# Five elementwise operations of the top-k bias, for blocks 1 to 4, on GpSimd instead of VectorE

## The chip, the core and the metric

The kernel runs on one core of a Trainium2 chip. The metric is the device time of one execution in microseconds, the median of the runs shown.

## What is computed

One layer of a hybrid decoder. After an RMSNorm and one input projection, two groups of heads attend. The first is multi-head latent attention, dense and causal. The second is sparse: an indexer scores all keys, each query keeps its 256 best causal keys, and softmax attention runs over those alone. Then come the output projection, a residual, a SwiGLU feed-forward network with its residual, and a last RMSNorm. The part that matters here is the choice of the keys:

```python
score = jnp.where(causal[None], score, -jnp.inf)
_, sel = lax.top_k(score, topk)          # topk = 256
valid = sel <= qpos[None, :, None]
...
s = jnp.einsum('bqhd,bqkhd->bhqk', qb, k_sel, ...) * scale
s = jnp.where(valid[:, None], s, -jnp.inf)
p = jax.nn.softmax(s, axis=-1)
```

## The kernel before

There are 1024 tokens in eight query blocks of 128, and 16 meta tokens in front of the keys, so block b has 16 + 128(b+1) keys (`n_keys`). The kernel does not gather. For each block it turns the scores into a row of biases, 0 for a kept key and 1e30 for the others, and the attention scores of the sparse heads are all computed and get that bias (`scores`, L792). Block 0 needs only the causal bias.

**From scores to bias.** `idx_block` sums the eight indexer heads into `sc[b]` (128 x keys, fp32) and `keys` splits each score into an ordered high half `hi[b]` and low half `yb[b]`, both 16 bits wide and stored in the place of the score. `topk` then searches bit by bit: `search` counts in 16 steps how many high halves reach a trial value, L436 to L440 prepare the low halves of the ties, and a second search of 16 steps finds the low threshold `q`. Blocks 1 and 2 are searched together on VectorE (L397 to L406), blocks 3 and 4 one after the other on ScalarE (L382 to L385, with a last small step on GpSimd, L389 and L390).

**The end of `topk`**, L445 to L458, makes the bias once per block, on a block's 272 (block 1), 400, 528 or 656 (block 4) columns. L445 counts the keys above the low threshold and L446 takes them off what is needed. L448 marks low halves equal to `q`, L449 keeps those with the threshold's high half, L451 numbers them with a prefix sum, and L452 keeps the first `need` of them. L453 marks low halves above `q`, L454 adds both marks, L455 adds the high halves above the threshold, L457 turns a mark into 0 or 1e30, and L458 adds the causal bias to the last 128 columns. All are VectorE's. The tiles `e` and `g` and the search's own output (`jk`, from `junk`, L411) take turns in a ring of two buffers; the numbering of L451 lies in `g`, so L453 can write `g` only after L452 has read it.

**Order.** Nothing of the order is written by hand: the program is given to a scheduler that fixes each engine's queue when the kernel is built, by its own estimate of when things are ready. Each engine then works through its queue in order and waits at its head.

The stages, by the time at which they run in the profiled execution:
- to about 328 us the projections. `run` (L588) works through seven column groups of the input matrix, each for eight row blocks, in a ring of seven PSUM banks once the first groups are done; ScalarE copies the products out, VectorE rotates them (`rope`, L334 to L336), GpSimd adds the halves (L338) and takes the low parts of the weights (L191). Top-k of blocks 1 to 4 is mixed into this stage by `fill` (`TOPK`, L47), and ends in the next.
- from about 328 us the latent projections and attention of blocks 0 to 2 (`CFG_A`). Their sparse heads read the biases of blocks 1 and 2, copied at L970; those of blocks 3 and 4 are copied at L1327 and first read by the second attention.
- from about 500 to 1050 us three streams side by side: the attention of blocks 3 to 7 (`CFG_B`), the feed-forward network of blocks 0 to 2 (`ffn`), and the top-k of blocks 5 to 7 (`TOPK_B`, `DEFER`).
- then the output projection and the feed-forward network of blocks 3 to 7, to the end.

Of the kernel before, what the change touches and what calls it, by code (L numbers as in the profile page):

```python
# [19 lines left out]
OP = mybir.AluOpType  # L20
# [6 lines left out]
P = 128  # L27
# [3 lines left out]
NK = NM + T  # L31
# [16 lines left out]
DEFER = (5, 6, 7)  # L48
# [35 lines left out]
BIG = 1e30  # L84
# [6 lines left out]
def n_keys(b):  # L91
    return NM + P * (b + 1)
# [13 lines left out]
def hybrid_layer(ctx, tc, a, out):  # L106
    nc = tc.nc
    V, S, G, PE = nc.vector, nc.scalar, nc.gpsimd, nc.tensor
# [20 lines left out]
    cbias = cp.tile([P, NK], BF, name="cbias")  # L129
# [102 lines left out]
    yb = {b: sc[b].bitcast(U16)[:, n_keys(b):2 * n_keys(b)] for b in sc}  # L232
# [7 lines left out]
    with ExitStack() as es:  # L240
# [170 lines left out]
        def junk(n):  # L411
            return wk_pool[0].tile([P, NK], BF, name="jk", bufs=2)[:, :n]
# [11 lines left out]
        def topk(blocks, on_act):  # L424
# [17 lines left out]
            q = yield from search(blocks, yb, 32768.0, w[:, 4:8], on_act, thr[:, 1:2] if on_act else need)  # L442
            for b, c, n in cols:
                yield
                V.tensor_scalar(junk(n), yb[b], q[:, c], None, op0=OP.is_gt, op1=OP.add, accum_out=cnt[:, c])  # L445
                V.tensor_sub(need[:, c], need[:, c], cnt[:, c])  # L446
                e, g = junk(n), junk(n)
                V.tensor_scalar(e, yb[b], q[:, c], None, op0=OP.is_equal)  # L448
                V.scalar_tensor_tensor(e, hi[b], Th[:, c], e, op0=OP.is_equal, op1=OP.mult)  # L449
                rk = g.bitcast(F16)  # L450
                V.tensor_tensor_scan(rk, e, e, 0.0, OP.add, OP.bypass)  # L451
                V.scalar_tensor_tensor(e, rk, need[:, c], e, op0=OP.is_le, op1=OP.mult)  # L452
                V.tensor_scalar(g, yb[b], q[:, c], None, op0=OP.is_gt)  # L453
                V.tensor_add(e, e, g)  # L454
                V.scalar_tensor_tensor(g, hi[b], Th[:, c], e, op0=OP.is_gt, op1=OP.add)  # L455
                bb = yb[b].bitcast(BF)
                V.tensor_scalar(bb, g, -BIG, BIG, op0=OP.mult, op1=OP.add)  # L457
                V.tensor_tensor(bb[:, n - P:n], bb[:, n - P:n], cbias[:, NK - P:NK], op=OP.add)  # L458
                yield

        def start(groups, on_act, steps):
# [197 lines left out]
    op = ctx.enter_context(tc.tile_pool(name="oh", bufs=1))  # L659
# [647 lines left out]
    with aa_es:  # L1307
        work = attention(aa, BLK_A, cfg)
        rest = mla_rest()
        n = 0  # L1310
# [57 lines left out]
    for x, y in ((ckH, ckL), (wkH, wkL)):  # L1368
        n = x.shape[1] // WO_W
# [55 lines left out]
```

## Time and profile before

| | |
|---|---|
| median of 3 runs | 1516.27 us (1514.63 to 1522.13) |
| profiled execution | 1515.98 us |
| its span in the trace | 1514.2 us |
| TensorE matmul busy | 1405.1 us, 93% |
| VectorE busy | 1105.3 us, 73% |
| ScalarE busy | 922.9 us, 61% |
| GpSimd busy | 892.8 us, 59% |

The span is from the first to the last instruction of the core; the execution's own time holds 1.8 us more. Busy times of engines overlap. A group of instructions in the profile is told by its line in the kernel, its engine, what it writes from what it reads, and its shape; the idle time beside it is that of its engine just before. PE is TensorE, DVE VectorE, ACT ScalarE, POOL GpSimd.

### The profile page before, as it was taken

What the parts mean: (1) busy time and instruction counts of PE and PEld (TensorE: products, weight loads), DVE (VectorE), ACT (ScalarE), POOL (GpSimd) and SP (SyncE); (2) the same over time, 40 slices, a digit from 0 to 9 for tenths busy, and PEclk for the clock granted to TensorE, in tenths of its full rate; (3) what the DMA queues carried; (4) which work ended last, traced back from release to release, by engine and by line L of the source; (5) the groups of instructions that cost most, each with busy time, mean ns of one, the idle gap of its engine ahead of it and who ended that gap; (6) DMA issues with size and microseconds to landing.
All of it is one profiled execution on the core that took longest, in us unless ns stands there. A gap on an engine that the chain in (4) does not pass through costs nothing. (4 is left out here: it accounts for less than half of the span.)

```text
span 1514.2 us, 29979 instructions
## 1 busy us (share of the span) xinstructions
PE 1405.1 (93%) x10320; PEld 1295.3 (86%) x10320; DVE 1105.3 (73%) x2714; ACT 922.9 (61%) x2264; POOL 892.8 (59%) x1185
## 2 busy tenths in 40 slices
PE   6999998899989899899999999888799999999996
PEld 5999998897778789798888888788789999999995
DVE  6878989948886875957766666736676777777766
ACT  5666578897889889788544444434544444444444
POOL 2564555212404588687878778643846666666653
PEclk9999999999999799999999999998899999999999
DMA  6113265224434688687879998741222222222211
GB/s 177 55 48 85 73 143 134 52 89 131 130 102 123 146 193 166 147 171 175 182 157 222 200 203 181 188 140 50 65 62 84 84 84 84 79 76 83 84 56 70
DMA packets 353737, 180.74 MB, mean 119 GB/s; under 512 B 196560, under 2 KB 341344, under 8 KB 353584
## 3 DMA queue, kind: packets, MB, share of 16 engines
q1 hardware_dynamic: 353584, 178.82, 47.7%
q8 instruction: 81, 1.33, 0.4%
q14 instruction: 72, 0.59, 0.1%
HBM read 120.77 MB, written 21.30 MB: 94 GB/s over the span
## 5 line engine op out<-in xcount | busy, mean ns | idle before, releaser
L191 POOL TENSOR_TENSOR wL<-raw,wH 128x256 fp32r<-128x256 f32 x352 | 286.1, 846 | 59.0 <-ACT wH L188 55.3
L821 POOL TENSOR_TENSOR hl<-pd,hl 128x260 f16<-128x260 f32 (+5 forms) x256 | 168.8, 689 | 71.1 <-ACT hl L817 31.8
L191 POOL TENSOR_TENSOR wsl<-raw,wsh 128x256 fp32r<-128x256 f32 x132 | 120.3, 940 | 94.1 <-ACT wsh L188 53.6
L196 PE MATMUL b<-wh,uH 128*128 128x256 f32 (+3 forms) x568 | 169.2, 298 | 6.3 <-DVE mlo L318 3.2
L198 PE MATMUL b<-wh,uL 128*128 128x256 f32 (+3 forms) x568 | 168.5, 297 | 0.0
L197 PE MATMUL b<-wl,uH 128*128 128x256 f32 (+3 forms) x568 | 168.1, 296 | 0.1
L188 ACT ACTIVATE wH<-raw 128x1024 fp32r<-128x1024 f32 x88 | 91.8, 1054 | 79.4 <-PE b L198 20.0
L196 PE MATMUL b<-us,wsh 128*128 128x320 f32 x440 | 136.1, 313 | 1.5 <-DVE oh L1251 1.1
L197 PE MATMUL b<-us,wsh 128*128 128x320 f32 x440 | 136.4, 311 | 0.0
L198 PE MATMUL b<-us,wsl 128*128 128x320 f32 x440 | 134.2, 310 | 0.0
L196 PE MATMUL b<-ua,wH 128*128 128x384 f32 x352 | 122.1, 347 | 3.4 <-ACT wH L188 3.4
L382 ACT ACTIVATE js<-sc,bs 128x528 bf16<-128x528 int16 (+7 forms) x128 | 120.9, 945 | 4.7 <-DVE sc L437 2.4
L197 PE MATMUL b<-ua,wH 128*128 128x384 f32 x352 | 121.2, 344 | 0.0
L198 PE MATMUL b<-ua,wL 128*128 128x384 f32 x352 | 120.7, 344 | 0.1
L196 PE MATMUL b<-wH,hH 128*128 128x512 f32 x282 | 113.5, 403 | 3.9 <-DVE oh L1171 2.1
L196 PEld LDWEIGHTS b<-wh,uH 128*128 128x128 f32 x568 | 108.7, 191 | 8.3 <-DVE mlo L318 3.9
L197 PE MATMUL b<-wL,hH 128*128 128x512 f32 x282 | 112.1, 397 | 0.0
L198 PE MATMUL b<-wH,hL 128*128 128x512 f32 x282 | 110.1, 398 | 0.4 <-DVE hL L193 0.4
L197 PEld LDWEIGHTS b<-wl,uH 128*128 128x128 f32 x568 | 108.8, 191 | 0.5 <-DVE wl L193 0.3
L198 PEld LDWEIGHTS b<-wh,uL 128*128 128x128 f32 x568 | 108.6, 191 | 0.4 <-DVE uL L193 0.2
L1240 DVE TENSOR_TENSOR oh<-b,oh 128x512 f32<-128x512 f32 x110 | 74.5, 685 | 46.3 <-PE b L198 45.4
L799 ACT ACTIVATE pd<-pd,sm 128x528 f32<-128x528 f32 (+4 forms) x80 | 75.7, 946 | 48.6 <-DVE sm L797 46.1
(410 smaller groups left out, 4848.0 us busy)
## 6 DMA issues: line engine op xcount, KB each, us to landing
raw<-in_w_gate SPq DMA_DIRECT2D x44, 512.0 KB, 4.0
raw<-in_w_up SPq DMA_DIRECT2D x44, 512.0 KB, 4.1
raw<-in_w_down SPq DMA_DIRECT2D x44, 512.0 KB, 3.7
wor<-in_w_o SPq DMA_DIRECT2D x64, 128.0 KB, 2.5
wraw<-in_w_in SPq DMA_DIRECT2D x40, 128.0 KB, 2.4
vh<-v_x SPq DMA_DIRECT2D x16, 288.0 KB, 3.8
xt<-in_x SPq DMA_DIRECT2D x8, 512.0 KB, 4.4
ks_x<-st SPq DMA_DIRECT2D x32, 128.0 KB, 2.1
```

The source lines that it names most:

```text
L188: S.activation(h, src, AF.Copy)
L191: G.tensor_sub(l[:, c], src[:, c], h[:, c])
L196: PE.matmul(o, lh, rh, start=first, stop=False, **kw)
L197: PE.matmul(o, lh, rl, start=False, stop=False, **kw)
L198: PE.matmul(o, ll, rh, start=False, stop=last, **kw)
L382: S.activation(act_junk()[:, :n_keys(b)], y[b], AF.Sign, bias=cols[0], accum_out=cnt)
L799: S.activation(pb, pb, AF.Exp, bias=mn, scale=-1.0, accum_out=z)
L821: G.tensor_sub(pl_[:, c], pb[:, c], ph[:, c])
L1240: V.tensor_add(oh[t][:, cs], po, oh[t][:, cs])
```

## The change

An engine `E` is chosen per block: VectorE for the deferred blocks 5 to 7, GpSimd for blocks 1 to 4. L448, L453, L454, L457 and L458 are given to `E`. The operations and their operands stay the same. The two lines that are added shift the line numbers behind them by 2.

```diff
             for b, c, n in cols:
                 yield
+
+                E = V if b in DEFER else G
                 V.tensor_scalar(junk(n), yb[b], q[:, c], None, op0=OP.is_gt, op1=OP.add, accum_out=cnt[:, c])
                 V.tensor_sub(need[:, c], need[:, c], cnt[:, c])
                 e, g = junk(n), junk(n)
-                V.tensor_scalar(e, yb[b], q[:, c], None, op0=OP.is_equal)
+                E.tensor_scalar(e, yb[b], q[:, c], None, op0=OP.is_equal)
                 V.scalar_tensor_tensor(e, hi[b], Th[:, c], e, op0=OP.is_equal, op1=OP.mult)
                 rk = g.bitcast(F16)
                 V.tensor_tensor_scan(rk, e, e, 0.0, OP.add, OP.bypass)
                 V.scalar_tensor_tensor(e, rk, need[:, c], e, op0=OP.is_le, op1=OP.mult)
-                V.tensor_scalar(g, yb[b], q[:, c], None, op0=OP.is_gt)
-                V.tensor_add(e, e, g)
+                E.tensor_scalar(g, yb[b], q[:, c], None, op0=OP.is_gt)
+                E.tensor_add(e, e, g)
                 V.scalar_tensor_tensor(g, hi[b], Th[:, c], e, op0=OP.is_gt, op1=OP.add)
                 bb = yb[b].bitcast(BF)
-                V.tensor_scalar(bb, g, -BIG, BIG, op0=OP.mult, op1=OP.add)
-                V.tensor_tensor(bb[:, n - P:n], bb[:, n - P:n], cbias[:, NK - P:NK], op=OP.add)
+                E.tensor_scalar(bb, g, -BIG, BIG, op0=OP.mult, op1=OP.add)
+                E.tensor_tensor(bb[:, n - P:n], bb[:, n - P:n], cbias[:, NK - P:NK], op=OP.add)
                 yield
```

The scheduler makes new queues from this, so more moves than twenty instructions. On all engines the queues are the same up to block 3's bias, differ by a few places to about 360 us, are the same again to about 500 us, and differ from there to about 1050 us, where most instructions of TensorE, VectorE, ScalarE, GpSimd and the DMA queue stand some places from where they stood. Behind that they are the same. Three places:

VectorE's queue at the end of block 3's bias (`sc_104`; `rq` and `mlo` belong to the projections, `sc_102` and `sc_103` to the search of blocks 1 and 2). Before:

```order
L452 SCALAR_TENSOR_TENSOR jk<-jk,bs_3215 128x528
L334 TENSOR_TENSOR rq_4186<-st,rope_73 128x256
L335 TENSOR_TENSOR rq_4187<-st,rope_73 128x4x32
L336 TENSOR_TENSOR rq_4187<-st,rope_73 128x4x32
L453 TENSOR_SCALAR jk<-sc_104,bs_3215 128x528
L318 TENSOR_TENSOR mlo<-b_4220,mlo 16x256
L454 TENSOR_TENSOR jk<-jk 128x528
L455 SCALAR_TENSOR_TENSOR jk<-sc_104,bs_3215,jk 128x528
L334 TENSOR_TENSOR rq_4242<-st,ropem 16x256
L335 TENSOR_TENSOR rq_4243<-st,ropem 16x4x32
L336 TENSOR_TENSOR rq_4243<-st,ropem 16x4x32
L457 TENSOR_SCALAR sc_104<-jk 128x528
```

and after the change:

```order
L454 SCALAR_TENSOR_TENSOR jk<-jk,bs_3215 128x528
L334 TENSOR_TENSOR rq_4186<-st,rope_73 128x256
L335 TENSOR_TENSOR rq_4187<-st,rope_73 128x4x32
L336 TENSOR_TENSOR rq_4187<-st,rope_73 128x4x32
L318 TENSOR_TENSOR mlo<-b_4220,mlo 16x256
L334 TENSOR_TENSOR rq_4242<-st,ropem 16x256
L335 TENSOR_TENSOR rq_4243<-st,ropem 16x4x32
L336 TENSOR_TENSOR rq_4243<-st,ropem 16x4x32
L457 SCALAR_TENSOR_TENSOR jk<-sc_104,bs_3215,jk 128x528
L397 TENSOR_SCALAR jk,bs_3201<-sc_102,bs_3201 128x272
L397 TENSOR_SCALAR jk,bs_3201<-sc_103,bs_3201 128x400
L404 TENSOR_TENSOR bs_3201<-bs_3201 128x2
```

The three operations L453, L454 and L457 are gone from between the projections' work, and L455 (now L457) stands behind all of it, with the search of blocks 1 and 2 right behind.

GpSimd's queue at the same place (`st` is the projections' rotated rows, `wl` the low parts of weights). Before:

```order
L390 TENSOR_TENSOR bs_3215<-bs_3215 128x1
L338 TENSOR_TENSOR st<-rq_4111,rq_4112 128x256
L338 TENSOR_TENSOR st<-rq_4186,rq_4187 128x256
L338 TENSOR_TENSOR st<-rq_4242,rq_4243 16x256
L191 TENSOR_TENSOR wl<-wraw,wh 128x256 x3
L338 TENSOR_TENSOR st<-rq_4277,rq_4278 128x256
L191 TENSOR_TENSOR wl<-wraw,wh 128x256
```

and after the change:

```order
L390 TENSOR_TENSOR bs_3215<-bs_3215 128x1
L450 TENSOR_SCALAR jk<-sc_104,bs_3215 128x528
L338 TENSOR_TENSOR st<-rq_4111,rq_4112 128x256
L455 TENSOR_SCALAR jk<-sc_104,bs_3215 128x528
L338 TENSOR_TENSOR st<-rq_4186,rq_4187 128x256
L456 TENSOR_TENSOR jk<-jk 128x528
L338 TENSOR_TENSOR st<-rq_4242,rq_4243 16x256
L459 TENSOR_SCALAR sc_104<-jk 128x528
L191 TENSOR_TENSOR wl<-wraw,wh 128x256 x2
L460 TENSOR_TENSOR sc_104<-sc_104,cbias 128x128
L191 TENSOR_TENSOR wl<-wraw,wh 128x256
```

Five operations of block 3 now stand one by one between the additions of the projections (L338) and the weights' low parts (L191).

VectorE's queue where the search of blocks 5 (`sc_67`) and 6 (`sc_68`) begins in the second attention (`pd` and `sm` are scores and their row minima, `kL` and `qL` the low parts of keys and queries). Before:

```order
L792 ISA sm 128x1
L193 TENSOR_TENSOR kL_7507<-b_8628,kH_7506 64x348
L792 ISA pd,sm<-b_8623,cbias,sm 128x456
L792 ISA sm 128x1
L436 TENSOR_SCALAR jk,bs_7874<-sc_68,bs_7874 128x912
L437 SCALAR_TENSOR_TENSOR sc_68<-sc_68,bs_7874 128x912
L397 TENSOR_SCALAR jk,bs_7864<-sc_67,bs_7864 128x784
L797 TENSOR_SCALAR sm<-sm 128x1
L438 TENSOR_SCALAR bs_7874<-bs_7874 128x1
L193 TENSOR_TENSOR kL_7507<-b_8667,kH_7506 64x344
L792 ISA pd,sm<-b_8662,cbias 128x348
```

and after the change:

```order
L794 ISA sm 128x1
L794 ISA pd,sm<-b_8623,cbias,sm 128x456
L794 ISA sm 128x1
L799 TENSOR_SCALAR sm<-sm 128x1
L193 TENSOR_TENSOR kL_7507<-b_8667,kH_7506 64x344
L193 TENSOR_TENSOR qL<-b_8682,qH 96x512
L1159 SCALAR_TENSOR_TENSOR sg<-sg,b_12420 128x384
L794 ISA pd,sm<-b_8662,cbias 128x348
L794 ISA sm 128x1
L794 ISA pd,sm<-b_8673,cbias,sm 128x348
L794 ISA sm 128x1
L436 TENSOR_SCALAR jk,bs_7874<-sc_68,bs_7874 128x912
```

The wide operations L436, L437 and L397 of that search stood ahead of a block's last small step on its minima (L797, now L799); now that step, two low parts, a step of the feed-forward network and the next block's minima come first.

## Rows read from the trace of the kernel before

**Rows 1.** The page: the span, and each engine's busy time, share and instructions.

```profile
span 1514.2 us, 29979 instructions
...
PE 1405.1 (93%) x10320; PEld 1295.3 (86%) x10320; DVE 1105.3 (73%) x2714; ACT 922.9 (61%) x2264; POOL 892.8 (59%) x1185
```

**Rows 2.** Busy time of the engines by stretch. Columns: the stretch, its length, then for PE, PEld, DVE, ACT and POOL the busy us with instructions in brackets, TensorE's granted clock, DMA share, GB/s.

```profile
255.00:303.00 48.00, 42.41 (x342) 41.59 (x341) 44.34 (x146) 39.08 (x114) 15.61 (x22) 0.96 0.33 75
303.00:330.00 27.00, 26.94 (x229) 26.54 (x227) 9.15 (x31) 24.87 (x71) 0.40 (x2) 1.00 0.15 47
330.00:360.00 30.00, 26.34 (x148) 21.66 (x149) 26.45 (x72) 23.57 (x67) 9.27 (x26) 0.89 0.44 134
...
500.00:1050.00 550.00, 512.95 (x4216) 466.40 (x4217) 369.46 (x924) 343.84 (x771) 406.46 (x566) 0.97 0.77 171
```

**Rows 3.** Groups of VectorE's instructions between 255 and 360 us, the five that the change moves, all widths of blocks 1 to 4 together: busy us, mean ns of one, idle us before.

```profile
L454 DVE TENSOR_TENSOR jk<-jk 128x528 bf16<-128x528 bf16 (+3 forms) x4 | 1.8, 450 | 0.1
...
L448 DVE TENSOR_SCALAR jk<-sc,bs 128x528 bf16<-128x528 uint16 (+3 forms) x4 | 1.3, 337 | 0.0
L453 DVE TENSOR_SCALAR jk<-sc,bs 128x528 bf16<-128x528 uint16 (+3 forms) x4 | 1.3, 328 | 0.0
...
L457 DVE TENSOR_SCALAR sc<-jk 128x528 bf16<-128x528 bf16 (+3 forms) x4 | 1.1, 270 | 0.0
...
L458 DVE TENSOR_TENSOR sc<-sc,cbias 128x128 bf16<-128x128 bf16 x4 | 1.0, 258 | 0.0
```

**Rows 4.** Timeline of VectorE around block 3's bias: start, us, instruction.

```profile
264.83 0.35 DVE L448 TENSOR_SCALAR jk<-sc,bs 128x528 bf16<-128x528 uint16 x1
265.10 0.42 DVE L334 TENSOR_TENSOR rq<-st,rope 128x256 f32<-128x256 f32 x1
265.43 0.28 DVE L335 TENSOR_TENSOR rq<-st,rope 128x128 f32<-128x128 f32 x1
...
266.70 1.67 DVE L451 TENSOR_TENSOR_SCAN jk<-jk 128x528 f16<-128x528 bf16 x1
...
269.84 0.35 DVE L453 TENSOR_SCALAR jk<-sc,bs 128x528 bf16<-128x528 uint16 x1
270.10 0.40 DVE L318 TENSOR_TENSOR mlo<-b,mlo 16x256 f32<-16x256 f32 x1
270.44 0.63 DVE L454 TENSOR_TENSOR jk<-jk 128x528 bf16<-128x528 bf16 x1
271.11 0.77 DVE L455 SCALAR_TENSOR_TENSOR jk<-sc,bs,jk 128x528 bf16<-128x528 int16 x1
...
272.53 0.28 DVE L457 TENSOR_SCALAR sc<-jk 128x528 bf16<-128x528 bf16 x1
...
273.15 0.39 DVE L458 TENSOR_TENSOR sc<-sc,cbias 128x128 bf16<-128x128 bf16 x1
```

**Rows 5.** Groups of GpSimd's instructions in the whole execution, shapes apart: busy us, mean ns of one, idle us before and what ended it.

```profile
L1002 POOL TENSOR_SCALAR woh<-wor 128x256 fp32r<-128x256 f32 x12 | 10.1, 853 | 6.7 <-PE b L832 6.3 <-DMA wor<-in_w_o 0.2
...
L1003 POOL TENSOR_TENSOR wol<-wor,woh 128x256 fp32r<-128x256 f32 x12 | 8.5, 732 | 0.0
...
L744 POOL TENSOR_TENSOR q_a<-qr,qr 128x128 f32<-128x128 f32 x6 | 2.7, 463 | 0.4 <-DVE qr L743 0.2 <-ACT q_a L738 0.2
...
L389 POOL TENSOR_SCALAR bs<-bs 128x1 f32<-128x1 f32 x8 | 1.8, 222 | 18.6 <-ACT bs L383 18.6
```

**Rows 6.** Timeline of VectorE, two rows, and of GpSimd, one row, at 256 us: start, us, instruction, count.

```profile
256.83 0.84 DVE L334 TENSOR_TENSOR rq<-st,rope 128x256 f32<-128x256 f32 x1
257.60 0.83 DVE L335 TENSOR_TENSOR rq<-st,rope 128x128 f32<-128x128 f32 x1
...
255.96 2.32 POOL L191 TENSOR_TENSOR wl<-wraw,wh 128x256 fp32r<-128x256 f32 x3
```

**Rows 7.** What TensorE waited for on VectorE, the first two rows from 255 to 303 us, the last two from 330 to 360 us: us in total, times, longest us.

```profile
PE b L196 <- DVE mlo L318: 3.0, 2, 2.0
PE b L196 <- DVE vw L168: 1.5, 1, 1.5
...
PE b L790 <- DVE kL L193: 0.4, 1, 0.4
...
PE b L790 <- DVE qL L193: 0.2, 1, 0.2
```

**Rows 8.** Timeline of VectorE where the second search begins, and the next wait of TensorE for a transposed block of probabilities (idle us before it, and what ended it).

```profile
512.50 1.15 DVE L436 TENSOR_SCALAR_CACHE_REDUCE jk<-sc,bs 128x912 bf16<-128x912 int16 x1
...
513.58 1.32 DVE L437 SCALAR_TENSOR_TENSOR sc<-sc,bs 128x912 uint16<-128x912 int16 x1
514.82 1.02 DVE L397 TENSOR_SCALAR_CACHE_REDUCE jk<-sc,bs 128x784 bf16<-128x784 int16 x1
...
515.77 0.14 DVE L797 TENSOR_SCALAR sm<-sm 128x1 f32<-128x1 f32 x1
...
517.53 0.23 PE L830 MATMUL b<-vh,pT 128*128 128x64 f16 x1 [1.92 <-DMA pT<-hl]
```

**Rows 9.** Busy time by stretch of 50 us from 500 to 1050 us: the stretch in which TensorE lost least, the one in which it lost most, and sum and mean of all eleven. Columns as in rows 2.

```profile
550.00:600.00 50.00, 49.56 (x414) 45.51 (x414) 25.96 (x74) 46.25 (x106) 40.15 (x62) 1.00 0.81 176
600.00:650.00 50.00, 43.97 (x355) 39.08 (x354) 46.59 (x106) 39.22 (x86) 37.10 (x45) 1.00 0.65 141
...
sum 550.00, PE 512.95 PEld 466.40 DVE 369.46 ACT 343.84 POOL 406.46; mean PE 46.63 PEld 42.40 DVE 33.59 ACT 31.26 POOL 36.95
```

## Prediction

> **What bounds the kernel now.** The page comes first [rows 1]: TensorE is busy 93% of the span, VectorE 73%, GpSimd 59%. So VectorE's time counts only where TensorE waits for it. The stretches say where that may be [rows 2]. The biases of blocks 3, 1 and 2 are made in the first of these stretches, that of block 4 in the third. From 255 to 303 us VectorE is nearly full, 44.34 of 48 us, and TensorE loses 5.6. From 303 to 330 us VectorE has 17.9 us free and TensorE loses nothing. From 330 to 360 us VectorE is at 26.45 of 30, and TensorE loses 3.7. The waits name the share of VectorE in these losses [rows 7]: 3.0 us for `mlo` and 1.5 for `vw` in the first stretch, 0.4 and 0.2 for low parts of keys and queries in the third; the other rows of those stretches are ScalarE's. That is some 5 us in all, and no relief of VectorE in these stretches can bring more. The biases themselves are wanted late: those of blocks 1 and 2 by the sparse heads at the end of the first attention, those of blocks 3 and 4 in the second, behind 500 us.
>
> A measurement of this kernel can tell some 0.5% from no change, 7.6 us.
>
> **The change, part by part.**
>
> *Taken from VectorE:* five instructions in each of four blocks, 1.8 + 1.3 + 1.3 + 1.1 + 1.0 = 6.5 us [rows 3]. Block 3 alone gives 0.35 + 0.35 + 0.63 + 0.28 + 0.39 = 2.0 us [rows 4]; of the other 4.5 us block 4 has about 2 by its width.
>
> *Given to GpSimd:* no row shows these operations there on 16-bit data, so they go by the nearest ones [rows 5]. A TENSOR_SCALAR takes 222 ns for one column and 853 for 256, so 2.46 ns a column; a TENSOR_TENSOR takes 463 for 128 and 732 for 256, so 2.1 ns a column and 0.19 us. That gives for 272, 400, 528 and 656 columns 0.89, 1.21, 1.52 and 1.84 us for each of L448, L453 and L457, 0.77, 1.04, 1.31 and 1.58 for L454, and 0.46 for the 128 columns of L458. A block is three, one and one of these: 3.9, 5.1, 6.3 and 7.6 us, together 23 us for the 6.5. It is an estimate; GpSimd has the room, 15.6 busy us in the 48 and 9.3 in the 30 [rows 2]. As bounds I take VectorE's own durations (6.5 us) and half as much again as the estimate (35 us); the upper one makes block 3's waits below some 3 us longer. The Trainium skill (GPSIMD Engine Reference, section 4.1, Engine selection) would leave elementwise work on VectorE, and calls GpSimd roughly line-rate for one input and about twice as slow for two. The rows here put its one-input operation above its two-input one, 853 ns against 732 on 256 columns; by the page the three TENSOR_SCALARs would be the cheap ones, and the hand-overs below would shrink by about half.
>
> *Hand-overs.* A block's bias now crosses between the engines five times, and VectorE's queue holds other work behind each wait. Block 3, by the new queues: L449 waits for L448 on GpSimd, 1.52 us, while VectorE has three rotations beside it, 0.42 + 2 x 0.28 = 1.0 [rows 4]: 0.5 of waiting. L455 waits for L453, an addition of the projections in between, and L454, 1.5 + 0.7 + 1.3 = 3.5 us; VectorE has six rotations and `mlo` beside them, 2 x 1.0 + 0.4: 1.1 more. The second count of the search needs the buffer that L457 is still reading, 1.5 us, against a first count of 272 columns, some 0.5 (784 take 1.02 [rows 8]): 1.0. That is 2.6 us of waiting for 2.0 us of work saved, +0.6 for VectorE, nearly a wash. Behind these waits stand the search, whose result is wanted late, and rotations, whose results go out by DMA. What TensorE needs is `mlo` and `vw`. `mlo` (L318) stood behind L448 and L453 [rows 4], 0.7 us, and gains that, less the 0.5: -0.2 us. `vw` comes behind six more steps of the search, and may lose the 0.6 in part: +0.2.
>
> Blocks 1 and 2 have little work of others in between: VectorE waits up to 1.7 and 2.3 us for L453 and L454, and up to 0.9 and 1.2 for L448. I cost them at nothing, because 17.9 us of free VectorE follow [rows 2] and the seven banks of the projection hold the products that wait for VectorE; without that cover it is (3.9 + 5.1) - 2.5 = 6.5 us.
>
> Block 4 relieves a full VectorE by 2 us, at a place where TensorE waited 0.4 + 0.2 us for it [rows 7]. GpSimd's 1.84 + 1.58 us between L452 and L455 stand beside minima, rotations and low parts that stand in between in the new queue. I take -0.5, between 0 and -0.6.
>
> *Moved.* From about 500 us the queues are laid anew, though the change touches no instruction there. The one place that can be read off is the start of the search of blocks 5 and 6: L436, L437 and L397, 1.15 + 1.32 + 1.02 = 3.5 us, stood ahead of the step L797 of a block's minima, and now stand behind it [rows 8]. TensorE's next wait there was 1.92 us for transposed probabilities. I take -1.0, between 0 and -1.9. For the rest of the 550 us no sign can be read from a queue. It can be sized: eleven stretches of 50 us lost from 0.44 to 6.03 us of TensorE's time, 3.4 in the mean [rows 9], with a scatter of 1.8 us; eleven drawn anew would scatter by 1.8 x 3.3 = 6 us. I take 0 and keep 6 us to either side.
>
> *Sum:* -0.2 + 0.2 - 0.5 - 1.0 = -1.5 us. The profiled execution took 1515.98 us, its span 1514.2 and 1.8 around it; it lies 0.3 below the median of the runs. 1515.98 - 1.5 gives **1514.5 us**, the same within what can be measured.
>
> **The rivals.**
>
> *The new queues of the second attention decide it, for better.* For: the stretch is 550 us long, TensorE loses 37 us there, and in its best 50 us it lost 0.44 [rows 2, 9]; relieved early steps of minima are of the right kind. Against: the same work stands in it, and the moves are of some places only. At 10 us less lost than before, a little over one and a half of the scatter: 1504.5 us. It decides from 6 us beyond my sum, which a scatter of 6 passes in about one case of six, a little more for the place read off above: 0.21 with the parts of the first stages.
>
> *The same for worse:* 10 us more lost, 1524.5 us, and it counts as slower from 9 us beyond my sum: 0.07.
>
> *The hand-overs come through to TensorE.* Here the change is slower, by one mechanism: VectorE stands at L455 or L449 until GpSimd is done, and what TensorE needs is behind. The places are block 3, where VectorE is full, and block 4, where the next minima of the first attention stand behind the wait. If nothing ran beside GpSimd's 6.3 and 7.6 us, VectorE would lose 6.3 - 2.0 and 7.6 - 2.0 = 9.9 us, and all of it on TensorE gives 1515.98 + 9.9 = 1526 us; it decides from three quarters of that. A sharper form of it is seen in the trace: while GpSimd ran 2.32 us at L191, VectorE's L334 took 0.84 us where the same shape takes 0.42, and L335 0.83 [rows 4, 6]. About 1 us lost in 2.3, over 23 us of GpSimd, is up to 10 us of VectorE, against 6.5 saved. Against: the biases are not urgent, TensorE waits for VectorE rarely here, and the cover of 303 to 330 us takes what blocks 1 and 2 lose. The Trainium skill has the rule for this (GPSIMD Engine Reference, section 8, Key points): GpSimd shares its memory interfaces with VectorE, and contends with VectorE's instructions that have two inputs or a two-port mode. The stretched rows agree with it. Chance 0.10.
>
> *The relief goes nowhere:* GpSimd's work hides, VectorE's 6.5 us end as idle time, and the later queues bring neither good nor ill: 1516 us, within my forecast.
>
> **How the numbers follow.** Within 7.6 us of before, forecast and idle relief together: 0.62. Faster by over 0.5%: the better queues, 0.21. Slower by over 0.5%: hand-overs 0.10 and worse queues 0.07, 0.17. The range reaches from the better queues' 1504.5 to the edge of the hand-overs', 1504 to 1525 us; it leaves out the rest of both tails, about 2 in 10.
>
> **What would show it.** Right: five groups on GpSimd with some 23 us together; VectorE's busy time down by about 6 us; TensorE's losses up to 360 us within 2 us of 5.6, 0 and 3.7; the time from 360 to 500 us unchanged; what differs lies between 500 and 1050 us. Wrong: if VectorE idles for `jk` from GpSimd and TensorE's waits for `vw`, for copies of the projections or for `sm` at 350 us grow by several us, it was the hand-overs. If GpSimd's operations take 16-bit columns at another rate than 2.46 and 2.1 ns, the 23 us are wrong, and with them the waits of block 3. If the stretches to 360 us gain more than 5 us, TensorE had been held there by more than its waits tell.

## The result and the profile after

The changed kernel takes 1529.32 us in the median of six runs (1526.68 to 1539.88) against 1515.96 us before: a ratio of 1.0096, with 95% interval 1.0076 to 1.0116. The forecast was 1514.5 us, no change that can be measured. The profiled execution took 1532.62 us, its span 1530.8: 16.6 us more than before.

The page after, its span and busy times, against [rows 1]:

```profile
span 1530.8 us, 29964 instructions
...
PE 1410.3 (92%) x10320; PEld 1296.1 (85%) x10320; DVE 1098.2 (72%) x2694; ACT 924.5 (60%) x2264; POOL 913.3 (60%) x1205
```

VectorE lost 7.1 busy us and GpSimd gained 20.5. Twenty instructions changed engine. TensorE is busy 5.2 us longer with the same 10,320 instructions, so 11.4 of the 16.6 us are idle time.

GpSimd's groups of the five moved operations after, all four widths together (busy us, mean ns of one, idle before and what ended it), which answer to [rows 3]:

```profile
L455 POOL TENSOR_SCALAR jk<-sc,bs 128x528 bf16<-128x528 uint16 (+3 forms) x4 | 6.0, 1506 | 15.6 <-DVE jk L454 15.6
L450 POOL TENSOR_SCALAR jk<-sc,bs 128x528 bf16<-128x528 uint16 (+3 forms) x4 | 5.8, 1459 | 7.1 <-DVE bs L406 6.9
L456 POOL TENSOR_TENSOR jk<-jk 128x528 bf16<-128x528 bf16 (+3 forms) x4 | 4.5, 1121 | 0.1
L459 POOL TENSOR_SCALAR sc<-jk 128x528 bf16<-128x528 bf16 (+3 forms) x4 | 2.9, 725 | 1.4 <-DVE jk L457 1.2
L460 POOL TENSOR_TENSOR sc<-sc,cbias 128x128 bf16<-128x128 bf16 x4 | 1.7, 430 | 0.2
```

They sum to 20.9 us (23 were forecast). Line numbers after are larger by 2 from here on: L450 was L448, L460 was L458, and so is every later line.

What this did to the first stages is seen in the stretches of [rows 2], here after (stretch, length, busy us by engine, clock, DMA):

```profile
255.00:303.00 48.00, 42.39 (x336) 41.48 (x335) 40.50 (x126) 39.87 (x116) 25.13 (x32) 0.93 0.33 75
303.00:330.00 27.00, 25.76 (x219) 25.36 (x218) 10.51 (x31) 23.54 (x68) 4.10 (x6) 1.00 0.18 59
330.00:360.00 30.00, 27.01 (x144) 22.75 (x145) 23.82 (x64) 24.26 (x68) 15.62 (x30) 0.83 0.38 110
500.00:1050.00 550.00, 500.06 (x4070) 448.25 (x4071) 353.04 (x879) 335.61 (x738) 399.70 (x556) 0.97 0.75 170
```

TensorE loses 5.61, 1.24 and 2.99 us in the first three, where it lost 5.59, 0.06 and 3.66: half a microsecond in sum. In the fourth it loses 49.9 us, before 37.1. That is where most of the time went. The second stage, which opens with the transposes of `un`, begins as before. The rows of those transposes give the first and last start (first of the kernel before, then after):

```profile
L1068 PE MATMUL b<-ident,un x64: 270/362/476, 495.4 to 1068.4; 128*128 128x128 f32 x64
```
```profile
L1070 PE MATMUL b<-ident,un x64: 270/347/476, 495.6 to 1085.8; 128*128 128x128 f32 x64
```

The first is 0.2 us late, the last 17.4 us. So the whole loss is made between these two, in the second attention and the output projection behind it, where the change touches no instruction and only the order in the queues is new.

**Where the second attention stands still.** Its sparse heads (the heads that attend to the chosen keys alone) need the biases of blocks 5 to 7, which are searched during that stage; block 7's comes last. Timeline of VectorE around its end, before (minima L792, bias L458; start, us, instruction):

```profile
737.40 0.68 DVE L792 CUSTOM_DVE_ANT_0 pd<-b,sc,sm 128x456 f32<-128x456 f32 x1
...
759.39 0.64 DVE L458 TENSOR_TENSOR sc<-sc,cbias 128x128 bf16<-128x128 bf16 x1
759.95 0.50 DVE L792 CUSTOM_DVE_ANT_0 pd<-b,sc 128x348 f32<-128x348 f32 x1
```

and after (L794, L460):

```profile
740.13 0.69 DVE L794 CUSTOM_DVE_ANT_0 pd<-b,sc,sm 128x456 f32<-128x456 f32 x1
...
776.88 0.23 DVE L460 TENSOR_TENSOR sc<-sc,cbias 128x128 bf16<-128x128 bf16 x1
777.02 0.51 DVE L794 CUSTOM_DVE_ANT_0 pd<-b,sc 128x348 f32<-128x348 f32 x1
```

Behind block 6's minima (456 columns) the first sparse head can only go on with block 7, and its minima start the moment the bias is done. These scores stood for 22 us before and stand for 36 us after; block 7's bias ends at 777.1 us, not 760.0: 17.1 us late, about the whole loss.

**Why the bias is late.** Blocks 6 and 7 are searched one after the other on ScalarE, each in two searches; the first search is handed over by two small GpSimd instructions (L389, L390) to VectorE (L436). [rows 8] showed VectorE's end of the first hand-over before, at 512.50 us. After, GpSimd's timeline there, and at block 7's hand-over:

```profile
518.59 0.22 POOL L389 TENSOR_SCALAR bs<-bs 128x1 f32<-128x1 f32 x1
520.58 4.29 POOL L823 TENSOR_TENSOR hl<-pd,hl 128x260 f16<-128x260 f32 x7 [1.77 <-ACT hl L819]
524.83 0.19 POOL L390 TENSOR_TENSOR bs<-bs 128x1 f32<-128x1 f32 x1
...
684.73 0.20 POOL L389 TENSOR_SCALAR bs<-bs 128x1 f32<-128x1 f32 x1
684.90 2.36 POOL L823 TENSOR_TENSOR hl<-pd,hl 128x228 f16<-128x228 f32 x4
687.23 2.78 POOL L191 TENSOR_TENSOR wL<-raw,wH 128x256 fp32r<-128x256 f32 x4
689.97 0.50 POOL L390 TENSOR_TENSOR bs<-bs 128x1 f32<-128x1 f32 x1
```

and VectorE's, where the two counts start:

```profile
529.20 1.16 DVE L436 TENSOR_SCALAR_CACHE_REDUCE jk<-sc,bs 128x912 bf16<-128x912 int16 x1
...
695.64 1.25 DVE L436 TENSOR_SCALAR_CACHE_REDUCE jk<-sc,bs 128x1040 bf16<-128x1040 int16 x1
```

Before, GpSimd's rows of both hand-overs, and VectorE's of block 7, stood close together:

```profile
511.92 0.22 POOL L389 TENSOR_SCALAR bs<-bs 128x1 f32<-128x1 f32 x1 [1.36 <-ACT bs L383]
512.23 0.19 POOL L390 TENSOR_TENSOR bs<-bs 128x1 f32<-128x1 f32 x1
...
661.84 0.21 POOL L389 TENSOR_SCALAR bs<-bs 128x1 f32<-128x1 f32 x1
662.14 0.20 POOL L390 TENSOR_TENSOR bs<-bs 128x1 f32<-128x1 f32 x1
```
```profile
662.37 1.30 DVE L436 TENSOR_SCALAR_CACHE_REDUCE jk<-sc,bs 128x1040 bf16<-128x1040 int16 x1
```

From block 7's L389 to its L436 it took 0.5 us before, and 10.9 after: other subtractions were put between L389 and L390 on GpSimd, and minima, low parts and feed-forward sums ahead of L436 on VectorE. Block 6's hand-over takes 10.6 us, not 0.6. A chain of one ScalarE instruction after another, with two small hand-over steps of two tenths of a microsecond each, was cut open twice by 10 us.

The delays do not simply add up. Block 6's L389 was already 6.7 us late, and at its L436 the chain was 16.7 us late, of which 11.4 were left at its second hand-over. At block 7's L436 it was 33.3 us late, and 18.3 at the last hand-over, because the sixteen passes of block 7's second search took 60.8 us on ScalarE from first to last, and 76.0 before. GpSimd's rows of the second hand-overs of blocks 6 and 7, before and then after:

```profile
593.03 0.23 POOL L389 TENSOR_SCALAR bs<-bs 128x1 f32<-128x1 f32 x1
...
743.19 0.21 POOL L389 TENSOR_SCALAR bs<-bs 128x1 f32<-128x1 f32 x1 [0.45 <-ACT bs L383]
```
```profile
604.39 0.21 POOL L389 TENSOR_SCALAR bs<-bs 128x1 f32<-128x1 f32 x1
...
761.52 0.21 POOL L389 TENSOR_SCALAR bs<-bs 128x1 f32<-128x1 f32 x1
```

The bias's 17.1 us are what remains of all this. This account of the lateness is read from the two traces; no kernel was run in which the hand-overs alone were moved.

### The profile page after: what moved, and what is told of

The parts are those of the page before. It is cut to its first block, busy times and chain, and to the rows that moved or that the text cites. A ratio compares the mean times of both kernels' runs of the same rounds, so it can differ in the third digit from the quotient of the medians.

```text
span 1530.8 us, 29964 instructions
## 1 busy us (share of the span) xinstructions
PE 1410.3 (92%) x10320; PEld 1296.1 (85%) x10320; DVE 1098.2 (72%) x2694; ACT 924.5 (60%) x2264; POOL 913.3 (60%) x1205
## 4 chain that ended last, share of the span: by engine, by line
PE 40%; DVE 19%; DMA 9%; POOL 8%; ACT 7%; issue 5%; SPq 1%; DVEq 0%; ACTq 0%; POOLq 0%
PE b L196 12%; PE b L198 11%; PE b L197 11%; POOL wL L191 4%; DVE jk L397 3%; PE b L792 3%; DMA pT<-hl 2%; POOL hl L823 2%; ACT js L382 2%; DMA raw<-in_w_up 2%; DMA wor<-in_w_o 2%; DMA raw<-in_w_gate 1%; DVE pd L794 1%; DMA raw<-in_w_down 1%; DVE bs L406 1%
## 5 line engine op out<-in xcount | busy, mean ns | idle before, releaser
L191 POOL TENSOR_TENSOR wL<-raw,wH 128x256 fp32r<-128x256 f32 x352 | 282.7, 836 | 69.3 <-ACT wH L188 61.9
L191 POOL TENSOR_TENSOR wsl<-raw,wsh 128x256 fp32r<-128x256 f32 x132 | 120.3, 939 | 95.0 <-ACT wsh L188 54.5
```

Of the source, the lines that this page charges most:

```text
L191: G.tensor_sub(l[:, c], src[:, c], h[:, c])
```

## The experiments

The table has every kernel that ran. "Order" is that of the queues from 500 us on: B as before, A as after (A' nearly), other letters for others; in the two "hold" kernels it holds up to the output projection. The next columns are from the profiled execution: when the last of the three biases ends, when the last product of probabilities and values starts, and the time. Then the median, and the ratio to the kernel before, which ran beside it, with its 95% interval.

| kernel | moved | order | bias | values | profiled | median | ratio, 95% |
|---|---|---|---|---|---|---|---|
| before | 0 | B | 760.0 | 966.0 | 1516.0 | 1514.6 to 1516.3 | 1 |
| the change | 20 | A | 777.1 | 984.6 | 1532.6 | 1529.3 | 1.0096, 1.0076 to 1.0116 |
| e1_b23 | 10 | B | 764.1 | 971.5 | 1521.1 | 1515.2 | 0.9999, 0.9986 to 1.0013 |
| e1_b2 | 5 | A' | 776.4 | 983.6 | 1531.7 | 1533.1 | 1.0130, 1.0108 to 1.0152 |
| e1_b4 | 5 | C | 762.1 | 969.8 | 1519.5 | 1514.9 | 1.0002, 0.9978 to 1.0027 |
| e1_19of20 | 19 | C | 768.4 | 978.5 | 1526.4 | 1510.7 | 0.9997, 0.9972 to 1.0022 |
| e2_one | 1 | A' | 776.1 | 987.0 | 1534.0 | 1534.3 | 1.0120, 1.0090 to 1.0150 |
| e2_before_late | 0 | near B | 762.7 | 969.2 | 1520.2 | 1516.0 | 1.0000, 0.9983 to 1.0018 |
| e2_after_late | 20 | near A | 780.0 | 971.7 | 1520.6 | 1521.3 | 1.0043, 1.0023 to 1.0062 |
| e2_after_half | 20 | other | 751.9 | 947.6 | 1506.0 | 1511.7 | 0.9982, 0.9964 to 0.9999 |
| e3_before_7v | 0 | D | 762.7 | 965.5 | 1520.3 | 1520.3 | 1.0030, 1.0014 to 1.0045 |
| e3_after_7v | 20 | D | 763.8 | 967.9 | 1518.9 | 1514.8 | 1.0002, 0.9985 to 1.0019 |
| e3_before_6v | 0 | other | 759.1 | 975.0 | 1525.7 | 1526.1 | 1.0069, 1.0051 to 1.0088 |
| e3_after_6v | 20 | other | 767.3 | 969.1 | 1521.3 | 1521.2 | 1.0042, 1.0026 to 1.0058 |
| e4_after_hold | 20 | A | 772.4 | 978.9 | 1526.1 | 1531.1 | 1.0131, 1.0104 to 1.0159 |
| e4_before_hold | 0 | B | 763.3 | 973.6 | 1520.5 | 1513.0 | 0.9991, 0.9978 to 1.0005 |
| e4_before_56v | 0 | E | 702.9 | 974.8 | 1535.2 | 1531.2 | 1.0109, 1.0092 to 1.0127 |
| e4_after_56v | 20 | E | 693.0 | 970.0 | 1531.9 | 1532.3 | 1.0128, 1.0110 to 1.0147 |
| e5_before_12 | 0 | B to the bias | 782.0 | 984.6 | 1536.1 | 1536.6 | 1.0149, 1.0131 to 1.0167 |
| e5_block7_gpsimd | 5 | B to the bias | 773.5 | 982.3 | 1533.9 | 1530.6 | 1.0095, 1.0072 to 1.0119 |

A profiled execution can lie off its median (19 of 20: 1526.4 against 1510.7), so kernels are compared by the ratio. It comes from all runs of both and need not be the quotient of the medians: the twelve runs of 19 of 20 spread from 1508.1 to 1526.4 us, those of block 4 alone, in the same order C, from 1507.0 to 1524.6.

### Is it GpSimd's work, or the order?

Theory: the order from 500 us on makes the loss. Rival: GpSimd's operations and the waits for them. The order comes out of a scheduler, and jumps with small edits: so part of the change can be had with the old order, and a small part of it with the new one.

```
e1_b23     - E = V if b in DEFER else G
           + E = G if b in (2, 3) else V
e1_b2      + E = G if b == 2 else V
e1_b4      + E = G if b == 4 else V
e1_19of20  - E.tensor_tensor(bb[:, n - P:n], bb[:, n - P:n], cbias[...
           + (E if b > 1 else V).tensor_tensor(bb[:, n - P:n], bb[:, n - P:n], cbias[...
e2_one     (on the kernel before)
           - V.tensor_scalar(bb, g, -BIG, BIG, op0=OP.mult, op1=OP.add)
           + (G if b == 1 else V).tensor_scalar(bb, g, -BIG, BIG, op0=OP.mult, op1=OP.add)
```

Expected of blocks 2 and 3:

> Operations moved for blocks 2 and 3 alone, ten of the twenty, among them block 3's, which stand in the fullest stretch. From 500 us on the queues of all five engines are row for row those of the kernel before. Queue theory (the loss is made by the new queues of the second attention): 1514 to 1517 us, ratio 0.998 to 1.001. Hand-over theory (the loss is what GpSimd's operations and the waits for them cost): about half of the 13.4 us, 1521 to 1525 us. Block 7's bias should end at 759 us, as before, by the first and later by the second.

Expected of block 2 alone:

> Operations moved for block 2 alone, five of the twenty. From 500 us on the queues are nearly those of the full change (94 of some 1,400 VectorE rows stand elsewhere, by at most 7 places). Queue theory: the whole loss with a quarter of the work, 1526 to 1531 us, and block 7's bias ends at 775 to 779 us. Hand-over theory: a quarter of the loss, 1517 to 1520 us.

Expected of block 4 alone, and of nineteen of twenty:

> Operations moved for block 4 alone, five of the twenty. From 500 us on the queues are neither those of before nor those of the full change, a third order. Queue theory: any time from 1505 to 1535 us, and the same as that of the kernel with nineteen of twenty operations moved, which has the same third order. Hand-over theory: a quarter of the loss, 1517 to 1520 us.

> Nineteen of the twenty operations moved; only the addition on 128 columns of block 1 stays on VectorE. From 500 us on the queues have the third order of the kernel with block 4 alone (four rows of TensorE differ). Queue theory: within 2 us of the kernel with block 4 alone, whatever that takes. Hand-over theory: the whole loss, 1528 to 1531 us, and some 10 us above the kernel with block 4 alone.

Expected of one operation:

> One operation of the twenty moved: block 1's multiply-add on 272 columns, 0.4 us. From 500 us on the queues are nearly those of the full change (155 of some 1,400 VectorE rows stand elsewhere, by at most 7 places). Queue theory: the whole loss, 1527 to 1533 us, and block 7's bias ends at 775 to 779 us of the span. Hand-over theory: under 1 us of loss, 1514 to 1517 us.

Measured: ten operations in the old order cost nothing (0.9999), nineteen in a third order cost nothing (0.9997), five in the new order cost 1.30%, and one single operation of 0.4 us in the new order costs 1.20%, all that the full change costs. So the loss follows the order, and the rival falls. Three details missed the forecasts: the kernels with five and with one operation lie 2.1 and 1.3 us above the ranges given for them, and the medians of the two kernels in order C are 4.2 us apart, not 2; their ratios agree. The bias of block 7 with ten operations moved, and with one (timelines of VectorE):

```profile
763.42 0.64 DVE L460 TENSOR_TENSOR sc<-sc,cbias 128x128 bf16<-128x128 bf16 x1
```
```profile
739.82 0.69 DVE L794 CUSTOM_DVE_ANT_0 pd<-b,sc,sm 128x456 f32<-128x456 f32 x1
...
775.91 0.23 DVE L460 TENSOR_TENSOR sc<-sc,cbias 128x128 bf16<-128x128 bf16 x1
776.06 0.51 DVE L794 CUSTOM_DVE_ANT_0 pd<-b,sc 128x348 f32<-128x348 f32 x1
```

### Is the late bias the cause?

First, the wait was filled, and the bias brought forward. In the "late" kernels the first sparse head's block 7 is scored in the second sparse head, behind that head's block 6:

```
+ seq, ahead = [(b, h, passes, v) for b in cfg["order"]], cfg["ahead"]
+ if b0 and half and h == 0:
+     late = seq.pop()
+ if b0 and half and h == 1:
+     seq.insert(4, late)
+     ahead = 5
...
e2_after_half
- S.activation(act_junk()[:, :n_keys(b)], y[b], AF.Sign, ...
+ S.activation(act_junk()[:, :n_keys(b) // (2 if b == 7 else 1)],
+              y[b][:, :n_keys(b) // (2 if b == 7 else 1)], AF.Sign, ...
```

> The kernel before, with one step put off: the first sparse head of the second attention leaves out block 7, which is taken in the second sparse head, behind that head's blocks 3 to 6. Everything is computed. Gate theory (the sparse heads stand still until block 7's bias is done, 22 us in the kernel before): four more scores can run in the wait, 10 to 18 us are gained, 1497 to 1506 us, and the end of block 7's bias no longer sets the span, which ends less than 750 us behind it. Rival, by which the end of the bias only marks a lateness that comes from elsewhere: 1512 to 1518 us, 754 us behind it as before.

> The full change with the same step put off. Everything is computed. Gate theory: the wait is 36 us here, four more scores fill up to 20 of it, 1508 to 1518 us. Rival (the lateness comes from elsewhere): 1526 to 1533 us.

> The full change, with ScalarE's search passes of block 7 over 520 of its 1040 columns; the other half is left out, and so are up to 32 x 0.56 us of ScalarE. The queues from 500 us on are laid anew. Gate theory: block 7's bias ends 2 to 18 us earlier, and the span ends 753 to 757 us behind that end as in the six traces so far, so 1512 to 1529 us. Rival (no such tie): the span does not follow that end, above 758 or below 752 us.

In the kernel with the change the filled wait gives back 8 us, a ratio of 1.0043 in place of 1.0096; by the forecast it was to give back 11 us or more. The bias ends no earlier there, but the minima go on to 759 us (timeline of VectorE):

```profile
758.62 0.68 DVE L794 CUSTOM_DVE_ANT_0 pd<-b,sc,sm 128x456 f32<-128x456 f32 x1
...
779.66 0.30 DVE L460 TENSOR_TENSOR sc<-sc,cbias 128x128 bf16<-128x128 bf16 x1
779.88 0.51 DVE L794 CUSTOM_DVE_ANT_0 pd<-b,sc 128x348 f32<-128x348 f32 x1
```

The half search leaves out half of block 7's keys, so it does not compute the layer. It brings the bias forward by 25 us, and all of the loss is gone (0.9982). This alone does not show the cause, for ScalarE has less work there and the later queues are new; the span ended 752.4 us behind the bias, just outside the 753 to 757 of the forecast. But my forecast for the kernel before was wrong: filling its 22 us gave nothing (1.0000), where 10 to 18 us were expected. There the wait is free. As I read it, TensorE takes in the feed-forward of the first blocks meanwhile: the last of its gate and up products starts at 961.7 us, some four before the last values (rows of these products, first and last start, before and then after):

```profile
L196 PE MATMUL b<-ua,wH x352: 331/338/668, 515.0 to 961.7; 128*128 128x384 f32 x176
```
```profile
L196 PE MATMUL b<-ua,wH x352: 332/338/525, 513.0 to 963.1; 128*128 128x384 f32 x176
```

Before, both kinds of work end together. After, the feed-forward ends where it did, and the attention goes on alone for 21 us, to 984.6. By this reading a bias later than 760 us costs, and an earlier one brings little; the second half rests on the half search alone.

Then the bias alone was delayed, in the kernel before, with every queue as it was up to that point:

```
e5_before_12      + for _ in range(13 if b == 7 else 1): V.scalar_tensor_tensor(e, hi[b], Th[:, c], e, ...
e5_block7_gpsimd  + E = G if b == 7 else V
```

> The kernel before, with one operation of block 7's bias (the product of the two comparisons, which leaves its input as it is when repeated) done thirteen times, not once; the result is the same. The queues of all engines are those of before up to this operation, which started at 747 us. 12 x 1.30 = 15.6 us more in block 7's bias. Late-bias theory (the sparse heads wait for this bias, and what TensorE does in the wait is not given back): the bias ends at 773 to 778 us, and the time goes up by 12 to 16 us, to 1527 to 1531 us, as far as the full change. Rival (the harm is done by the new order of the work between 500 and 740 us, which is that of before here): 1514 to 1520 us.

> The kernel before, with the five operations of block 7 alone on GpSimd, none of blocks 1 to 4. The queues are those of before up to block 7's bias at 744 us. By the rates of the full change (2.7 to 2.9 ns a column for the comparisons, 2.2 for the addition, 1.1 for the multiply-add) 1040 columns take 2.9 + 2.9 + 2.3 + 1.2 + 0.4 = 9.7 us there in place of 3.2 on VectorE. Late-bias theory: the bias ends 6 to 10 us later, 1520 to 1526 us. Rival (as above): 1513 to 1518 us.

Delayed by 22.0 us (the repeats took longer than 1.30 each, and other work came between), the time rose by 21.8. Delayed by 13.5 us, on GpSimd, it rose by 15.8: five operations on one of the blocks that the change leaves out cost as much as all that it moves. Timeline of GpSimd in that kernel:

```profile
744.38 2.96 POOL L450 TENSOR_SCALAR jk<-sc,bs 128x1040 bf16<-128x1040 uint16 x1
757.21 2.93 POOL L455 TENSOR_SCALAR jk<-sc,bs 128x1040 bf16<-128x1040 uint16 x1
762.84 2.17 POOL L456 TENSOR_TENSOR jk<-jk 128x1040 bf16<-128x1040 bf16 x1
771.92 1.06 POOL L459 TENSOR_SCALAR sc<-jk 128x1040 bf16<-128x1040 bf16 x1
773.07 0.43 POOL L460 TENSOR_TENSOR sc<-sc,cbias 128x128 bf16<-128x128 bf16 x1
```

Both times are above what was expected, because the bias came later than expected; against the delay itself the price is about 1 to 1. So a late bias is enough to make the loss, without anything new between 500 and 740 us. The rival, that the end of the bias only marks a lateness from elsewhere, falls. One doubt is left: in both kernels the queues from the bias on are new too, and what that order costs is not told apart from the delay. Two executions with the same queues from 500 us on speak for the delay: in block 4 alone and 19 of 20 the bias ended at 762.1 and 768.4 us, and they took 1519.5 and 1526.4.

### What of the work drawn ahead?

A third account was that TensorE's queue after has 906 thousand columns between the start of the stage and the last values, not 882: products of the output projection that are drawn ahead of the attention's tail. A count that can be made in the queue alone would be worth having. Three edits of the search's table gave other counts, and a kernel that holds the projection's transposes back until the last outputs are there tried it directly:

```
e3_..._7v   TOPK_B = [([[7]], False, 2), ([[5], [6]], True, 3)]
e3_..._6v   TOPK_B = [([[6]], False, 2), ([[5], [7]], True, 3)]
e4_..._56v  TOPK_B = [([[5], [6]], False, 4), ([[7]], True, 3)]
e4_..._hold
+ idt = ident
+ if blocks[-1] == NB - 1:
+     idt = wo.tile([P, P], F32, name="idt")
+     V.tensor_scalar(idt[:, 0:1], oh[NB - 1][:, D - 1:D], 0.0, None, op0=OP.mult)
+     V.tensor_scalar(idt, ident, idt[:, 0:1], None, op0=OP.add)
...
- PE.transpose(pt[...], oh[t][...], ident)
+ PE.transpose(pt[...], oh[t][...], idt)
```

> The kernel before, with block 7 searched on VectorE and blocks 5 and 6 on ScalarE (before: 5 on VectorE, 6 and 7 on ScalarE). Everything is computed. Work-ahead theory (the time follows how many columns of TensorE's queue stand between the start of the second stage and the last values of the second attention; measured so far: 861 thousand gave 1511.7 us, 882 gave 1515, 894 gave 1521, 906 gave 1529 to 1534): 869 thousand here, so 1511 to 1515 us. Without such a tie, anything from 1505 to 1530 us.

> The same edit on the full change, all twenty operations on GpSimd. From 500 us on its queues are nearly those of the other (17 of some 1,400 VectorE rows stand elsewhere, by at most 3 places), with 869 thousand columns too. Queue theory: the change costs nothing here, within 3 us of the other kernel, 1510 to 1516 us. Hand-over theory: some 13 us above the other.

> The kernel before, with block 6 searched on VectorE and blocks 5 and 7 on ScalarE; no operation on GpSimd. The count of columns ahead of the last values is 901 thousand. Work-ahead theory: 1515 us and 0.66 us for each thousand above 882, so 1523 to 1531 us, slower than before by about as much as the full change is. Without the tie: the change is not there, so 1510 to 1520 us.

> The full change, all twenty operations on GpSimd, with block 6 on VectorE and blocks 5 and 7 on ScalarE. 876 thousand columns. Work-ahead theory: 1511 to 1516 us, faster than the same edit without the change by 8 to 18 us. Hand-over theory: slower than that one by some 13 us.

> The full change; the transposes that open the output projection of blocks 3 to 7 wait for block 7's last outputs (their identity matrix is made with a zero taken from them). Everything is computed. The queues are those of the full change up to the end of the second attention (TensorE's first 9,119 of 12,434 instructions); 9.6 thousand columns of the output projection move from before the last values to behind them. Work-ahead theory (what is drawn ahead of the last values delays them, and is not given back behind them): about 6 us back, 1522 to 1527 us. Rival (that work only fills time in which TensorE would stand still): no gain, 1528 to 1535 us.

> The same edit on the kernel before, where only 0.5 thousand columns stand ahead of the last values: the price of the edit itself. Both theories: 1513 to 1518 us.

> The kernel before, with blocks 5 and 6 searched one after the other on VectorE in twice as large steps, and block 7 alone on ScalarE. Everything is computed. 856 thousand columns ahead of the last values. Work-ahead theory: below the kernel before, 1507 to 1515 us. Without the tie: 1510 to 1525 us.

> The same edit on the full change, all twenty operations on GpSimd. From 500 us on its queues are nearly those of the other (42 of some 1,400 VectorE rows stand elsewhere, by at most 8 places), 856 thousand columns too. Queue theory: within 5 us of the other, 1505 to 1515 us. Hand-over theory: some 13 us above the other.

Two kernels lie in the ranges that go with their count (1526.1 us for block 6 on VectorE without the change, 1514.8 for block 7 with it), four do not: 1520.3 and 1521.2 us where 1511 to 1516 were expected, and 1531.2 and 1532.3 for the 856 thousand columns that should have been the fastest. Holding the transposes back gave nothing (1.0131), and the edit itself costs nothing (0.9991). The account falls. In the kernels with blocks 5 and 6 on VectorE the last bias ends 57 and 67 us early and they are slow all the same: TensorE loses 40.4 us from 475 to 725 us in the one without the change, before 18.2. So the late bias is what these runs show as the cause of this change's loss, not the only way to lose in this stage.

Two pairs of these have nearly the same later queues with and without the twenty operations: 1.0030 and 1.0002, 1.0109 and 1.0128. By these the change itself is worth -0.3% and +0.2%, each uncertain by some 0.25%: no loss of its own is seen. The first pair was to agree within 3 us and lies 5.5 us apart. None of the kernels that compute everything beats the one before by 0.5%.

## Why the prediction was wrong

**What held.** GpSimd's 23 us (20.9; the comparisons took a little more than forecast, the multiply-add L459 2.9 us in place of 5.5), VectorE's 6.5 us less (7.1), `mlo` and `vw` (waits on VectorE of 3.0 and 1.5 us [rows 7], after 2.0 and 1.4), nothing lost or gained up to 500 us, and the loss all behind 500 us, up to the last transposes of `un`.

**Hand-overs.** Their end result, a wash, was right; the waits were not as worked out. In block 3 VectorE was to wait 2.6 us. Its timeline after, which answers to [rows 4]:

```profile
264.99 1.22 DVE L451 SCALAR_TENSOR_TENSOR jk<-sc,bs,jk 128x528 bf16<-128x528 int16 x1
...
270.40 0.83 DVE L334 TENSOR_TENSOR rq<-st,ropem 16x256 f32<-16x256 f32 x1 [0.60 <-ACT st L525]
271.16 1.27 DVE L335 TENSOR_TENSOR rq<-st,ropem 16x128 f32<-16x128 f32 x1
272.36 0.27 DVE L336 TENSOR_TENSOR rq<-st,ropem 16x128 f32<-16x128 f32 x1
272.56 0.75 DVE L457 SCALAR_TENSOR_TENSOR jk<-sc,bs,jk 128x528 bf16<-128x528 int16 x1
```

It waited for no result of GpSimd here. Instead two rotations took 0.83 and 1.27 us (0.41 and 0.27 before) while GpSimd ran L338 and L456. VectorE's waits for the moved operations in 255 to 400 us (us, times, longest) are of blocks 1 and 2, 3.4 us in all where up to 1.7 and 2.3, 0.9 and 1.2 were allowed for, and hidden as forecast:

```profile
DVE jk L457 <- POOL jk L456: 2.7, 2, 1.5
...
DVE jk L451 <- POOL jk L450: 0.7, 2, 0.4
```

**The step that failed: "Moved".** I had read the right place: L436 and L437, behind the first search of block 6, stood ahead of L797 before and behind it and others after [rows 8]. I took it as relief of the minima, "-1.0, between 0 and -1.9". The relief did not come: from 505 to 535 us TensorE waited 3.9 us for transposed probabilities, 2.8 before, and from 500 to 560 us it lost 8.3 us, before 5.8. And I had asked who is behind these instructions, and not what they lead to. L436 is a link of the chain that ends in block 7's bias: the searches of blocks 6 and 7 run one after the other, and the sparse heads wait for the end of the second. L436 of block 6 started at 529.20, not 512.50 us, 16.7 us late at the very place: 6.7 us had come before L389, 5.9 more on GpSimd up to L390, and 4.1 on VectorE, in the queue that I had read. So the term had the wrong sign, and a path that the sum did not have, the wait for block 7's bias, made the loss. That 16.7 and the bias's 17.1 are so near is chance: the second cut and the faster last search come between, and with block 2 alone this L436 was only 12.0 us late (524.52) and the loss no smaller.

**The size of the rest.** "I take 0 and keep 6 us to either side" treated eleven stretches [rows 9] as drawn one by one. They are not: one chain runs through them, and the delays made on purpose show that its end is paid for about 1 to 1. By stretches, TensorE's idle time before and after is 16.8 and 18.9 us (500 to 740), 3.5 and 2.6 (740 to 780, the wait itself), 7.4 and 11.6 (780 to 960), 4.7 and 4.7 (960 to 1000), 19.5 and 25.4 (1000 to 1125). The wait is not paid where it stands; TensorE has feed-forward to do there. It shows later, in the tail of the attention and the output projection behind it; that it is paid when the feed-forward is used up fits these rows and was not tried by itself. Nor are the two signs alike. The order before is a good one: of the eighteen other kernels that compute everything, the change among them, none gained 0.5%, and eleven lost 0.4 to 1.5%, two of them by a delay made on purpose. Many of these share an order, so they are not eighteen draws: order A, the two with block 6 on VectorE and order E are slower by 0.4 to 1.3%, C is not, D is by 0.3% in one kernel of two, and none is faster by 0.5%. I gave "better" 0.21 and "worse" 0.07; on this record the weights stood the wrong way round.

**The rivals.** The time of "hand-overs come through", 1526 us, was near the result, and its mechanism was not the cause: nineteen of the twenty operations ran at a ratio of 0.9997. The rival "the same for worse" named the right stretch and direction, but as a scatter without a cause, and its 1524.5 us too was short of the result.

**What stays open.** Why the last values come 203 to 211 us behind the bias in the kernels where the sparse heads wait for it (the half search, the filled wait and the other search tables apart), and why the 16.6 us show as 11.4 of idle and 5.2 of longer busy time, was not tried. So the way from the new queues to the late bias stays read from traces, for the search's hand-over was not made safe (L389 and L390 on VectorE, say) in the new order.

## What to carry to other kernels

When an edit makes a scheduler lay the queues anew, ask first which chain of small steps ends in a wait that everything behind needs, and follow its hand-overs in the new queues; a link of it that moves back can cost more than the room it makes for others. To tell an edit's own cost from that of the new order, look for parts of the edit that leave the order as it was, and for a trifle that brings the new one: ten operations of twenty cost nothing here, and one cost 1.2%. A wait that TensorE fills with other work may be free: filling one of 22 us gave nothing here, filling one of 36 us gave back 8.

## What the runs showed of the hardware

GpSimd's one-input operations were not alike. The comparison took 2.96 us for 1040 columns and 0.98 for 272; the multiply-add by constants 1.06 and 0.42 (with one of 1.11 for 400 columns); the addition of two inputs 2.17 for 1040. The rows of 272 columns, of the full change:

```profile
L450 POOL TENSOR_SCALAR jk<-sc,bs 128x272 bf16<-128x272 uint16 x1 | 1.0, 979 | 6.9 <-DVE bs L406 6.9
...
L459 POOL TENSOR_SCALAR sc<-jk 128x272 bf16<-128x272 bf16 x1 | 0.4, 421 | 0.6 <-DVE jk L457 0.6
```

My rates of 2.46 and 2.1 ns a column are near the slopes of the comparison (2.6 between these two widths) and of the addition (1.9); the multiply-add rises by 0.8 a column. The Trainium skill (GPSIMD Engine Reference, section 4.1, Engine selection) calls one-input operations on GpSimd roughly line-rate. The multiply-add is the nearest to that; the comparison, with its 2.96 us against 0.48 on VectorE (L448 of block 7 before), does not agree.

Some of VectorE's two-input operations were stretched beside GpSimd. L335 took 1.27 us on 16 x 128 while L456 ran on GpSimd (270.90 to 272.29 us), and its twin L336 behind it 0.27. The Trainium skill (GPSIMD Engine Reference, section 8, Key points) says that GpSimd contends with VectorE's instructions of two inputs; the rows agree. Up to 360 us TensorE's losses grew by half a microsecond only. Elsewhere the stretch was larger: L193 on 128 x 384 took 4.71 us at 685.71 us, while GpSimd worked through eight two-input operations (684.90 to 690.01 us), and 0.59 at 754.11, with GpSimd at work too; the rows do not show what decides.
